# Attention's half of an up-projection in Strassen units, that half first in every pair but the first, and gate rows scaled in the input projection

## The chip, the cores and the metric

The kernel runs on one core of a Trainium2 chip. The core has five engines with a queue each, run in the order of the program: TensorE (PE, with its weight loads listed as PEld), VectorE (DVE), ScalarE (ACT), GpSimd (POOL) and SyncE (SP), which here issues most DMA transfers. The metric is the device time of one execution in microseconds, the median of several runs. Matmuls write to PSUM, eight banks of 128 partitions x 512 float32 values; everything else lies in SBUF or in DRAM.

## The reference: one decoder layer

Float32 throughout, 512 tokens, model width 2048. The part that matters:

```
proj = rmsnorm(x) @ w_in                 # u, v_sgu, q, k, v: 1024 wide each; g_a, g_b: 2048 wide
y_a  = chunked_spatial_gating(gelu(u), rmsnorm(gelu(v_sgu)))
y_b  = stick_breaking_attention(rmsnorm(q), rmsnorm(k), v)
merged = sigmoid(g_a) * (y_a @ w_up_a) + sigmoid(g_b) * (y_b @ w_up_b)
x = x + merged @ w_o
x = x + (silu(gate) * up) @ w_ffn_out    # gate, up = rmsnorm(x) @ w_ffn_in
x = x + sigmoid(rmsnorm(x) @ w_ple_gate) * (p @ w_ple)
```

The norm of x is a factor of each token; the kernel multiplies it to the columns of `proj` afterwards, as `row1`.

## The kernel before

**Operands and units.** TensorE multiplies numbers of fewer bits than float32 has, so each operand is split into a high and a low part (`hi`, `lo`), and each product is three matmuls, high by high, high by low, low by high (`mm3`, lines L296 to L298). Activations lie with the token as the free dimension. A *unit* is 256 rows by 256 columns of weights against 512 tokens. A plain unit ("P") is 4 weight blocks x 3 = 12 matmuls of 512 columns. A Strassen unit ("S") computes seven products of sums of quarters instead of eight, each on 256 tokens: 7 x 3 = 21 matmuls of 256 columns. Where all units of a pair are Strassen units, `doubled` merges two of the three matmuls into one of 512 columns (L692); the input projection does so for five of the seven products, w_o and the FFN for all.

**Pairs.** A *pair* is a column block of 256 outputs: units over all rows of the input, accumulated in PSUM. A plain pair leaves its two halves in two banks (`ends()`). A Strassen pair sums its products into an SBUF tile (`mix`, by ScalarE copies L748 and VectorE sums, or `mix_doubled`, L751 and others); a mixed pair, with both kinds, adds its plain units' banks to that (`rest`, L796).

**Weights.** They come unit by unit or as two units at once (a *double*), in four steps: the load by SP (a plain double 512 KB; of a Strassen one 256 and 384 KB, and another 256 KB that GpSimd's queue adds onto the first in SBUF, L363); the high part by ScalarE (`whi`, L359); two sums of 256 for each Strassen unit by VectorE (L375); the low part by VectorE (`wlo`, L356). Three slots hold split weights. `prepare_early` and `prepare_late` push the next doubles through these steps from places inside a unit.

**Operands' forms.** A *form* turns an activation block of 256 rows into what TensorE reads: its high part by ScalarE (L286), its low part by VectorE (L287), both writing `parts`. A plain form does this for 1024 values of each partition. A Strassen form (`late_form`) is made plain first (`plain_first`), used so in the first pairs, and loaded a second time for the sums of quarters (L527) that its Strassen products need; from the pair number in a list like `HALF` on, a unit is a Strassen unit. A form is built by `tick()`, a counter that goes on once or twice in a unit and lets work start that is due (`after(n, ...)`: in n ticks; WAIT = 2 ticks for a load).

**Stages.** Input projection until 815.28 us: 28 pairs over eight blocks of x, in four rounds of q, k, v and some gate pairs, then s and u (the gating part) among the last gates. Attention's steps and those of the gating run beside it, called by ticks: in attention, L1134 writes a low part that matmul L1141 (a product with a triangle of ones) reads. A gate pair's 256 columns are stored to DRAM (`gsp`) as they are. Up-projection, 815.28 to 1004.59 us: for each of eight j, first attention's half (`b`, y_b from DRAM by `w_up_b[j]`), then the gating's half (`a`, y_a in SBUF by `w_up_a[j]`), four plain units each; five pairs also compute the small embedding product (`w_ple`), a plain unit each. For each half, the gate comes back from DRAM, is scaled by `row1` (L1224) and goes through the sigmoid (L1357), and the two banks are multiplied to it (L1362). The sum of both goes to DRAM as `mix`. Then w_o (eight pairs over the eight `mix` blocks, the first plain, the second mixed), the FFN in and out, and the last gate.

The order of instructions on each engine comes from the order in which the program issues them, with weights' steps at a higher priority.

Of the kernel before, what the change touches and what calls it, by code (L numbers as in the profile page):

```python
# [29 lines left out]
EPS = 1e-6  # L30
MASKED = -1e4

PASSES = "SSSSSSSS", "SSSSSSSS", "SSSSPP"
HALF = 1, 1, 1, 1, 2, 2, 2, 2
PLAIN_UNTIL = HALF, HALF, (2, 2, 2, 2, 1, 1)
# [35 lines left out]
def hybrid_layer(  # L71
# [28 lines left out]
    def nm(s):  # L100
        return f"{s}_{next(names)}"
# [509 lines left out]
                    src, far)  # L611

    def plain_form(src, ready=always, gain=None, raw=1024, how="low", far=False):
        def steps(form):
            hi, lo = form.blocks = parts.take(1024, how), parts.take(1024, how)
            w = form.raw()
            if gain:
                gained(hi.own(), w.f(), *gain)
                gi, k = gain
                for i in range(2):  # L620
                    a, b = i * T, (i + 1) * T
                    nc.vector.scalar_tensor_tensor(
                        out=lo.own(a, b), in0=w.f(a, b),
                        scalar=gcol[:, gi + 2 * k + i : gi + 2 * k + i + 1], in1=hi.f(a, b),
                        op0=ALU.mult, op1=ALU.subtract)
            else:
                split_into(hi.own(), lo.own(), w.f())
            give(w)
            return tuple([x.own(0, T), x.own(T)] for x in form.blocks)
            yield  # L630

        return Form("P", steps, [(parts, 1024, how)] * 2 + [(wholes, raw, "low")] * bool(raw),
                    ready, src, far)

    class Pair:
# [555 lines left out]
    def sgu_v(rnd, o):  # L1191

        for h in range(2):
# [18 lines left out]
            for t in range(NT):  # L1212
# [5 lines left out]
                scalar=gcol[:, g_sgu + g : g_sgu + g + 1],  # L1218
                in1=bb.unsqueeze(1).to_broadcast([P, NT, P]),
                op0=ALU.mult, op1=ALU.add)  # L1220

    def scaled(o, row):
        b = o.rearrange("p (b t) -> p b t", t=T)
# [49 lines left out]

    def plan_rest():
        for j in range(KU):
            for b in "ba":
                plan((w_up_a if b == "a" else w_up_b)[j], "PPPP")
            if 0 < j < 6:
                planned.append((w_ple[j + 2].rearrange("p (b c) -> p b c", b=4), 1, "P"))
        for j in range(KU):  # L1280
# [9 lines left out]
            plan(w_gate[j], now(GATE, GATE_UNTIL, j))  # L1290

    def y_form(c, i):
        return plain_form((lambda: y_a[i]) if c == "a" else lambda: load(y_spill[i]),
                          lambda: len(y_done) == 8, raw=0 if c == "a" else 1024,
                          far=c == "b")

    ys = {(c, i): y_form(c, i) for c in "ba" for i in range(4)}
    build(ys.values())
    for n, ((w, i), pr) in enumerate(zip(order, made())):
        if n == 0:  # L1300
# [19 lines left out]
        elif w == "u":  # L1320
            scaled(o, row1)
            nc.scalar.activation(o, o, AF.Gelu_apprx_tanh)
            nc.vector.tensor_tensor(out=y_a[i].f(), in0=o, in1=y_a[i].f(), op=ALU.mult)
            y_done["a", i] = True
        else:
            d = tc.dram_tile([P, 1024], F32, name=nm("gsp"))
            nc.sync.dma_start(out=d, in_=o)
            gate_spill[w, i] = d
    finish_waiting()
    give(*att.values())  # L1330


    part = {}
# [14 lines left out]
    ms = [spilled_form("S", "mix", j) for j in range(KU)]  # L1348
    build(ms)
    for j in range(KU):  # L1350
        for b in "ba":
            s = load(gate_spill[b, j], 1024, "low")
            g = s.f()

            def gate(g=g):
                scaled(g, row1)
                nc.scalar.activation(g, g, AF.Sigmoid)  # L1357

            after(1, gate)
            pr = pair([ys[b, i] for i in range(4)], last=j == KU - 1)  # L1360
            for h, ps in zip((g[:, :T], g[:, T:]), pr.ends()):
                nc.vector.tensor_tensor(out=h, in0=h, in1=ps, op=ALU.mult)  # L1362
            if b == "b":
                part[j] = s
            else:
                nc.vector.tensor_tensor(out=g, in0=g, in1=part[j].f(), op=ALU.add)
# [4 lines left out]
        elif j < 6:  # L1371
            ple_pair(j + 2)
            if j == 5:
                ple_done()
    give(norm1.block)


    norm2 = Norm()
    fs = [spilled_form("S", "x1", j, (g_ffn, j)) for j in range(KU)]
# [194 lines left out]
```

## Time and profile before

| | |
|---|---|
| median of 3 runs | 2658.71 us (2658.05 to 2658.91) |
| the profiled execution | 2659.74 us |
| its span, first to last instruction | 2658.0 us |
| mean granted TensorE clock | 0.999 |
| input projection | 0 to 815.28 us |
| up-projection | 815.28 to 1004.59 us |
| DMA traffic | 559.77 MB, mean 211 GB/s |

In a row of the timeline stand the start and the duration in microseconds, engine and line, the operation with what it writes and reads, and in brackets the idle time of the engine ahead of it with the instruction that ended it. In a group of instructions the count is followed by the busy time in us, the mean duration in ns, and the idle time ahead of them. In the table by stretches each engine has its busy time and the number of instructions; then come the granted clock, the busy share of the DMA engines and the rate that they moved.

### The profile page before, as it was taken

The numbers are of one execution on the slowest core, as the hardware profiler recorded it, in microseconds if no ns is written. First come the engines' busy times: TensorE is split into PE (matmuls) and PEld (weight loads), VectorE is DVE, ScalarE is ACT, GpSimd is POOL, SyncE is SP. The second block draws the span as 40 slices with busy tenths as digits, with TensorE's granted clock in tenths as the row PEclk, the third lists the DMA queues.
The fourth block names the chain that finished last, engine by engine and source line by source line (L and its number), as shares of the span: only waits on it lengthen the run. The fifth ranks groups of instructions, "written<-read, shape, count | busy, mean of one in ns | idle before, by whom it ended". The sixth has DMA issues, their size and how long they took to land.

```text
span 2658.0 us, 42554 instructions
## 1 busy us (share of the span) xinstructions
PE 2638.2 (99%) x15336; PEld 2312.3 (87%) x15336; DVE 2234.6 (84%) x3821; ACT 1403.2 (53%) x2233; POOL 448.1 (17%) x556
## 2 busy tenths in 40 slices
PE   8999999999999999999999999999999999999999
PEld 7888888888998888888888888888888888889898
DVE  8687878787886558999888888888889989989876
ACT  7756565655554334566444444444445445455543
POOL 0122222232220001101111111111110211211110
PEclk9999999999999999999999999999999999999999
DMA  7677777777775668978888888788887989978884
GB/s 229 162 194 171 192 173 191 172 191 179 178 191 183 232 212 268 265 236 218 223 210 216 206 200 203 194 209 204 199 207 221 257 227 273 229 229 260 256 240 123
DMA packets 293459, 559.77 MB, mean 211 GB/s; under 512 B 26368, under 2 KB 140544, under 8 KB 293248
## 3 DMA queue, kind: packets, MB, share of 16 engines
q1 hardware_dynamic: 231136, 441.95, 50.7%
q0 software_dynamic: 62112, 115.11, 27.5%
q8 instruction: 120, 1.97, 0.3%
q14 instruction: 91, 0.75, 0.1%
HBM read 505.57 MB, written 51.38 MB: 210 GB/s over the span
## 4 chain that ended last, share of the span: by engine, by line
PE 90%; DVE 4%; DMA 3%; issue 1%; ACT 1%; SPq 0%; POOL 0%; ACTq 0%; POOLq 0%; DVEq 0%
PE ps L692 53%; PE ps L298 10%; PE ps L297 9%; PE ps L296 9%; PE small L692 6%; DVE wlo L356 1%; DVE wholes L527 1%; DMA wholes<-w_ffn_out 1%; PE small L1103 1%; PE small L1155 1%; DVE parts L287 1%; PE small L1029 1%; DMA x<-wholes 1%; ACT whi L359 0%; PE small L1214 0%
## 5 line engine op out<-in xcount | busy, mean ns | idle before, releaser
L692 PE MATMUL ps<-parts,whi 128*128 128x512 f32 x4200 | 1409.4, 398 | 1.6 <-DVE out L796 1.0
L359 ACT ACTIVATE whi<-wholes 128x512 fp32r<-128x512 f32 (+2 forms) x940 | 871.5, 941 | 745.8 <-DVE wholes L375 286.6
L356 DVE TENSOR_TENSOR wlo<-wholes,whi 128x512 fp32r<-128x512 f32 (+2 forms) x940 | 979.4, 1076 | 73.7 <-ACT whi L359 73.0
L692 PEld LDWEIGHTS ps<-parts,wlo 128*128 128x128 f32 x4200 | 790.2, 188 | 178.2 <-issue 1.9
L692 PE MATMUL ps<-parts,wlo 128*128 128x256 f32 x4200 | 831.3, 279 | 0.9 <-DVE wlo L356 0.9
L692 PEld LDWEIGHTS ps<-parts,whi 128*128 128x128 f32 x4200 | 677.1, 189 | 10.5 <-issue 3.6
L297 PE MATMUL ps<-parts,whi 128*128 128x256 f32 (+1 forms) x1832 | 605.0, 331 | 0.7 <-DVE parts L287 0.5
L298 PE MATMUL ps<-parts,wlo 128*128 128x256 f32 (+1 forms) x1832 | 604.9, 331 | 0.5 <-DVE wlo L356 0.5
L296 PE MATMUL ps<-parts,whi 128*128 128x256 f32 (+1 forms) x1816 | 597.3, 330 | 7.4 <-ACT parts L286 5.3
L297 PEld LDWEIGHTS ps<-parts,whi 128*128 128x128 f32 x1832 | 347.0, 189 | 39.0 <-DVE parts L287 2.7
L296 PEld LDWEIGHTS ps<-parts,whi 128*128 128x128 f32 x1816 | 343.6, 190 | 40.4 <-ACT parts L286 5.7
L298 PEld LDWEIGHTS ps<-parts,wlo 128*128 128x128 f32 x1832 | 347.3, 190 | 32.4 <-DVE wlo L356 1.6
L375 DVE TENSOR_TENSOR wholes<-wholes 128x256 f32<-128x256 f32 (+1 forms) x820 | 345.0, 421 | 17.9 <-DVE wlo L356 1.4
L751 DVE TENSOR_TENSOR out<-out,ps 128x256 f32<-128x256 f32 x490 | 202.3, 416 | 147.6 <-ACT out L748 147.4
L363 POOL DMA_DIRECT2D wholes<-w_ffn_in x169 | 147.1, 870 | 702.1 <-DVE wholes L375 251.7
L363 POOL DMA_DIRECT2D wholes<-w_in x132 | 116.6, 885 | 531.3 <-DVE wholes L375 132.8
L692 PE MATMUL small<-parts,whi 128*128 128x512 f32 x480 | 190.3, 397 | 0.0
L287 DVE TENSOR_TENSOR parts<-wholes,parts 128x1024 fp32r<-128x1024 f32 (+3 forms) x137 | 122.8, 907 | 18.5 <-ACT parts L286 18.5
L286 ACT ACTIVATE parts<-wholes 128x1024 fp32r<-128x1024 f32 (+3 forms) x137 | 106.5, 800 | 54.2 <-DVE wholes L527 35.7
L748 ACT ACTIVATE out<-ps 128x256 f32<-128x256 f32 x258 | 96.3, 383 | 50.7 <-PE ps L692 46.7
L363 POOL DMA_DIRECT2D wholes<-w_ffn_out x64 | 55.7, 871 | 360.6 <-DMA wholes<-w_ffn_out 89.2
L1402 ACT ACTIVATE out<-out 128x512 f32<-128x512 f32 x44 | 27.9, 633 | 155.6 <-DVE out L1401 155.6
(124 smaller groups left out, 1770.0 us busy)
## 6 DMA issues: line engine op xcount, KB each, us to landing
wholes<-w_ffn_in SPq DMA_DIRECT2D x169, 384.0 KB, 5.5
wholes<-w_in SPq DMA_DIRECT2D x132, 384.0 KB, 5.1
wholes<-w_ffn_in SPq DMA_DIRECT2D x169, 256.0 KB, 4.7
wholes<-w_ffn_in POOLq DMA_DIRECT2D x169, 256.0 KB, 5.3
wholes<-w_in SPq DMA_DIRECT2D x132, 256.0 KB, 4.3
wholes<-w_in POOLq DMA_DIRECT2D x132, 256.0 KB, 5.0
wholes<-w_ffn_out SPq DMA_DIRECT2D x64, 384.0 KB, 6.3
wholes<-x SPq DMA_DIRECT2D x45, 512.0 KB, 5.8
```

Source lines behind the costliest of these rows:

```text
L286: return (nc.scalar.activation(hi, src, AF.Copy), nc.vector.tensor_tensor(out=lo, in0=src, in1=hi.bitcast(F32), op=ALU.subtract))
L287: nc.vector.tensor_tensor(out=lo, in0=src, in1=hi.bitcast(F32), op=ALU.subtract))
L296: nc.tensor.matmul(ps, sh, mh, start=start, stop=False)
L297: nc.tensor.matmul(ps, sh, ml, start=False, stop=False)
L298: return nc.tensor.matmul(ps, sl, mh, start=False, stop=stop)
L356: in_turn(nc.vector.tensor_tensor(out=self.lo[:, blocks], in0=r, in1=h.bitcast(F32), op=ALU.subtract))
L359: in_turn(nc.scalar.activation(h, r, AF.Copy))
L363: nc.gpsimd.dma_start(out=raw[:, 3:5], in_=self.src[:, 1:3], accum_op=ALU.add)
L375: in_turn(nc.vector.tensor_tensor(out=o, in0=x, in1=y, op=ALU.add))
L692: m = nc.tensor.matmul(out, l, r, start=first and k == 0, stop=last and k == 1)
L748: in_turn(nc.scalar.activation(out, x, AF.Copy, scale=scale))
L751: in_turn(nc.vector.tensor_tensor(out=out, in0=x, in1=y, op=op))
```

## The change

- The four forms of y_b become Strassen forms, loaded a second time. `UP_UNTIL = 1, 1, 2, 2`: the first two units of attention's half are plain in pair j = 0 and Strassen units from j = 1 on, the other two from j = 2 on. So j = 0 is plain, j = 1 mixed, j = 2 to 7 all Strassen, not doubled.
- Pair j = 0 has the gating's half first, all others attention's half; weights are planned in the same order. y_a's forms are built first, the first of them with one block at the other end of the arena.
- A Strassen pair's sum lies in an SBUF tile, and the gate is multiplied with it in one instruction of 1024 values; before, two read the banks.
- A gate pair is scaled by `row1` before it is stored, two ticks after its sum is there; at its load only the sigmoid is left, two ticks later.
- The input projection no longer ends by running all waiting steps (`finish_waiting()`); attention's tiles are given back in the last round of `sgu_v`, and the norm's block three ticks later.

```diff
--- before.py
+++ after.py
@@ -30,6 +30,7 @@
 EPS = 1e-6
 MASKED = -1e4
 
+UP_UNTIL = 1, 1, 2, 2
 PASSES = "SSSSSSSS", "SSSSSSSS", "SSSSPP"
 HALF = 1, 1, 1, 1, 2, 2, 2, 2
 PLAIN_UNTIL = HALF, HALF, (2, 2, 2, 2, 1, 1)
@@ -611,8 +612,10 @@
                     src, far)
 
     def plain_form(src, ready=always, gain=None, raw=1024, how="low", far=False):
+        hows = [how] * 2 if isinstance(how, str) else how
+
         def steps(form):
-            hi, lo = form.blocks = parts.take(1024, how), parts.take(1024, how)
+            hi, lo = form.blocks = [parts.take(1024, h) for h in hows]
             w = form.raw()
             if gain:
                 gained(hi.own(), w.f(), *gain)
@@ -629,7 +632,7 @@
             return tuple([x.own(0, T), x.own(T)] for x in form.blocks)
             yield
 
-        return Form("P", steps, [(parts, 1024, how)] * 2 + [(wholes, raw, "low")] * bool(raw),
+        return Form("P", steps, [(parts, 1024, h) for h in hows] + [(wholes, raw, "low")] * bool(raw),
                     ready, src, far)
 
     class Pair:
@@ -1218,6 +1221,10 @@
                 scalar=gcol[:, g_sgu + g : g_sgu + g + 1],
                 in1=bb.unsqueeze(1).to_broadcast([P, NT, P]),
                 op0=ALU.mult, op1=ALU.add)
+        if rnd == 3:
+            assert ("b", 3) in y_done
+            give(*att.values())
+            att.clear()
 
     def scaled(o, row):
         b = o.rearrange("p (b t) -> p b t", t=T)
@@ -1273,8 +1280,9 @@
 
     def plan_rest():
         for j in range(KU):
-            for b in "ba":
-                plan((w_up_a if b == "a" else w_up_b)[j], "PPPP")
+            for b in "ba" if j else "ab":
+                plan((w_up_a if b == "a" else w_up_b)[j],
+                     "PPPP" if b == "a" else now("SSSS", UP_UNTIL, j))
             if 0 < j < 6:
                 planned.append((w_ple[j + 2].rearrange("p (b c) -> p b c", b=4), 1, "P"))
         for j in range(KU):
@@ -1290,11 +1298,14 @@
             plan(w_gate[j], now(GATE, GATE_UNTIL, j))
 
     def y_form(c, i):
-        return plain_form((lambda: y_a[i]) if c == "a" else lambda: load(y_spill[i]),
-                          lambda: len(y_done) == 8, raw=0 if c == "a" else 1024,
-                          far=c == "b")
-
-    ys = {(c, i): y_form(c, i) for c in "ba" for i in range(4)}
+        def ready():
+            return len(y_done) == 8
+
+        if c == "a":
+            return plain_form(lambda: y_a[i], ready, raw=0, how="low" if i else ("high", "low"))
+        return late_form(lambda size=1024: load(y_spill[i], size), ready, far=True)
+
+    ys = {(c, i): y_form(c, i) for c in "ab" for i in range(4)}
     build(ys.values())
     for n, ((w, i), pr) in enumerate(zip(order, made())):
         if n == 0:
@@ -1323,11 +1334,14 @@
             nc.vector.tensor_tensor(out=y_a[i].f(), in0=o, in1=y_a[i].f(), op=ALU.mult)
             y_done["a", i] = True
         else:
-            d = tc.dram_tile([P, 1024], F32, name=nm("gsp"))
-            nc.sync.dma_start(out=d, in_=o)
-            gate_spill[w, i] = d
-    finish_waiting()
-    give(*att.values())
+            d = gate_spill[w, i] = tc.dram_tile([P, 1024], F32, name=nm("gsp"))
+
+            def spill_gate(o=o, d=d):
+                scaled(o, row1)
+                nc.sync.dma_start(out=d, in_=o)
+
+            after(2, spill_gate)
+    after(3, lambda: give(norm1.block))
 
 
     part = {}
@@ -1348,19 +1362,18 @@
     ms = [spilled_form("S", "mix", j) for j in range(KU)]
     build(ms)
     for j in range(KU):
-        for b in "ba":
+        for b in "ba" if j else "ab":
             s = load(gate_spill[b, j], 1024, "low")
             g = s.f()
-
-            def gate(g=g):
-                scaled(g, row1)
-                nc.scalar.activation(g, g, AF.Sigmoid)
-
-            after(1, gate)
-            pr = pair([ys[b, i] for i in range(4)], last=j == KU - 1)
-            for h, ps in zip((g[:, :T], g[:, T:]), pr.ends()):
-                nc.vector.tensor_tensor(out=h, in0=h, in1=ps, op=ALU.mult)
-            if b == "b":
+            after(2, lambda g=g: nc.scalar.activation(g, g, AF.Sigmoid))
+            pr = pair([ys[b, i] for i in range(4)], last=j == KU - 1, j=j,
+                      until=UP_UNTIL if b == "b" else None)
+            if pr.n["S"]:
+                tt(g, g, pr.out(), ALU.mult)
+            else:
+                for h, ps in zip((g[:, :T], g[:, T:]), pr.ends()):
+                    tt(h, h, ps, ALU.mult)
+            if j not in part:
                 part[j] = s
             else:
                 nc.vector.tensor_tensor(out=g, in0=g, in1=part[j].f(), op=ALU.add)
@@ -1372,8 +1385,6 @@
             ple_pair(j + 2)
             if j == 5:
                 ple_done()
-    give(norm1.block)
-
 
     norm2 = Norm()
     fs = [spilled_form("S", "x1", j, (g_ffn, j)) for j in range(KU)]
```

Lines move by one to a few: L356 becomes L357, L692 L695, L748 L751, L796 L799, L1134 L1137, L1141 L1144, L1224 L1231, L1357 L1368. Three places of the instruction order follow, each before and after the change.

**Attention, first round.** VectorE ahead of the low part that L1141 reads (L1134, after the change L1137). `wlo` is the weights' low part, `out` the sum of a gate pair. Before:

```order
L1147 TENSOR_TENSOR wholes<-wholes,small_2722 128x384
L356 TENSOR_TENSOR wlo_79<-wholes,whi_78 128x1280
L356 TENSOR_TENSOR wlo_79<-wholes,whi_78 128x512
L1134 TENSOR_TENSOR parts<-wholes,parts 128x512
L1112 SCALAR_TENSOR_TENSOR wholes<-wholes 128x128
```

After:

```order
L1150 TENSOR_TENSOR wholes<-wholes,small_2725 128x384
L357 TENSOR_TENSOR wlo_79<-wholes,whi_78 128x1280
L357 TENSOR_TENSOR wlo_79<-wholes,whi_78 128x512
L1231 TENSOR_TENSOR out_2632<-out_2632,wholes 128x1024
L1137 TENSOR_TENSOR parts<-wholes,parts 128x512
L1115 SCALAR_TENSOR_TENSOR wholes<-wholes 128x128
```

The scaling of a gate now stands ahead of the low part. TensorE at the same place; `small` is the bank of the masked sums, `tri` the triangle, `ps` the input projection's banks. Before:

```order
L692 MATMUL ps_2706<-parts,whi_80 128x512
L692 MATMUL ps_2706<-parts,wlo_81 128x256 x2
L692 MATMUL ps_2706<-parts,whi_80 128x512
L692 MATMUL ps_2717<-parts,whi_80 128x512
L1141 MATMUL small_2802<-parts,tri_123 128x512
L692 MATMUL ps_2717<-parts,wlo_81 128x256 x2
L692 MATMUL ps_2717<-parts,whi_80 128x512
L692 MATMUL ps_2735<-parts,whi_80 128x512
L692 MATMUL ps_2735<-parts,wlo_81 128x256 x2
L692 MATMUL ps_2735<-parts,whi_80 128x512
```

After:

```order
L695 MATMUL ps_2709<-parts,whi_80 128x512
L695 MATMUL ps_2709<-parts,wlo_81 128x256 x2
L695 MATMUL ps_2709<-parts,whi_80 128x512
L695 MATMUL ps_2720<-parts,whi_80 128x512
L695 MATMUL ps_2720<-parts,wlo_81 128x256 x2
L695 MATMUL ps_2720<-parts,whi_80 128x512
L695 MATMUL ps_2738<-parts,whi_80 128x512
L695 MATMUL ps_2738<-parts,wlo_81 128x256 x2
L695 MATMUL ps_2738<-parts,whi_80 128x512
L1144 MATMUL small_2807<-parts,tri_123 128x512
```

The masked sum, L1141 and now L1144, has moved behind seven more matmuls.

**Start of the up-projection, ScalarE.** L286 (now L287) writes the high parts of operands, in the 1024 form those of plain forms; `whi` is the weights' high part. Before:

```order
L286 ACTIVATE parts_73<-wholes_74 128x1024
L359 ACTIVATE whi1_78<-wholes_74 128x1024
L286 ACTIVATE parts_73<-wholes_74 128x1024
L359 ACTIVATE whi0_76<-wholes_74 128x1024
L1357 ACT_TABLE_LOAD
L1357 ACTIVATE wholes_74<-wholes_74 128x1024
L286 ACTIVATE parts_73<-wholes_74 128x1024 x2
L359 ACTIVATE whi2_80<-wholes_74 128x1024
L286 ACTIVATE parts_73<-wholes_74 128x1024 x2
```

After:

```order
L287 ACTIVATE parts_73<-wholes_74 128x1024 x3
L360 ACTIVATE whi2_80<-wholes_74 128x1024
L751 ACTIVATE out_783_8229<-ps_777_8099 128x256
L751 ACTIVATE out_783_8229<-ps_778_8104 128x256
L751 ACTIVATE out_783_8229<-ps_779_8109 128x256
L751 ACTIVATE p5_784_8234<-ps_780_8118 128x256
L287 ACTIVATE parts_73<-wholes_74 128x4x256
L360 ACTIVATE whi1_78<-wholes_74 128x1024
L287 ACTIVATE parts_73<-wholes_74 128x4x256 x2
L360 ACTIVATE whi0_76<-wholes_74 128x1024
L287 ACTIVATE parts_73<-wholes_74 128x4x256
L1368 ACT_TABLE_LOAD
```

Before, the first four 1024-wide operands are attention's, with the load of the sigmoid's table (ACT_TABLE_LOAD) ahead of the last of the others. Now the gating's four (three of them shown) come first, before the input projection's last sums (L751), then attention's, written in the layout of Strassen forms (4x256), and the table behind them all.

**w_o, second to third pair.** VectorE; L796 (now L799) adds a mixed pair's banks to its sum. Before:

```order
L356 TENSOR_TENSOR wlo_81<-wholes,whi_80 128x1280
L356 TENSOR_TENSOR wlo_81<-wholes,whi_80 128x512
L287 TENSOR_TENSOR parts<-wholes,parts 128x3x256
L375 TENSOR_TENSOR wholes<-wholes 128x256
L287 TENSOR_TENSOR parts<-wholes,parts 128x256
L375 TENSOR_TENSOR wholes<-wholes 128x256
L287 TENSOR_TENSOR parts<-wholes,parts 128x256
L796 TENSOR_TENSOR out_9665<-ps_9648,out_9665 128x512
L356 TENSOR_TENSOR wlo_79<-wholes,whi_78 128x1280
L356 TENSOR_TENSOR wlo_79<-wholes,whi_78 128x512
L796 TENSOR_TENSOR out_9665<-ps_9641,out_9665 128x512
```

After:

```order
L357 TENSOR_TENSOR wlo_81<-wholes,whi_80 128x1280
L528 TENSOR_TENSOR wholes<-wholes 128x256
L357 TENSOR_TENSOR wlo_81<-wholes,whi_80 128x512
L288 TENSOR_TENSOR parts<-wholes,parts 128x3x256 x2
L376 TENSOR_TENSOR wholes<-wholes 128x256
L288 TENSOR_TENSOR parts<-wholes,parts 128x256
L376 TENSOR_TENSOR wholes<-wholes 128x256
L288 TENSOR_TENSOR parts<-wholes,parts 128x256
L357 TENSOR_TENSOR wlo_79<-wholes,whi_78 128x1280
L357 TENSOR_TENSOR wlo_79<-wholes,whi_78 128x512
L799 TENSOR_TENSOR out_10071<-ps_10054,out_10071 128x512
L799 TENSOR_TENSOR out_10071<-ps_10047,out_10071 128x512
```

Both sums now stand behind the low parts of `wlo_79`; before, one stood ahead of them. TensorE; `whi_76` and `whi_80` are the weights of the pair's first and second double, each group of three rows is one product. Before:

```order
L692 MATMUL ps_9835<-parts,whi_76 128x512
L692 MATMUL ps_9835<-parts,wlo_77 128x256 x2
L692 MATMUL ps_9835<-parts,whi_76 128x512
L692 MATMUL ps_9844<-parts,whi_76 128x512
L692 MATMUL ps_9844<-parts,wlo_77 128x256 x2
L692 MATMUL ps_9844<-parts,whi_76 128x512
L692 MATMUL small_9854<-parts,whi_76 128x512
L692 MATMUL small_9854<-parts,wlo_77 128x256 x2
L692 MATMUL small_9854<-parts,whi_76 128x512
L692 MATMUL ps_9814<-parts,whi_80 128x512
L692 MATMUL ps_9849<-parts,whi_76 128x512
```

After:

```order
L695 MATMUL ps_10232<-parts,whi_80 128x512
L695 MATMUL ps_10232<-parts,wlo_81 128x256 x2
L695 MATMUL ps_10232<-parts,whi_80 128x512
L695 MATMUL ps_10237<-parts,whi_80 128x512
L695 MATMUL ps_10237<-parts,wlo_81 128x256 x2
L695 MATMUL ps_10237<-parts,whi_80 128x512
L695 MATMUL ps_10248<-parts,whi_80 128x512
L695 MATMUL ps_10248<-parts,wlo_81 128x256 x2
L695 MATMUL ps_10248<-parts,whi_80 128x512
L695 MATMUL ps_10257<-parts,whi_76 128x512
L695 MATMUL ps_10257<-parts,wlo_77 128x256 x2
L695 MATMUL ps_10257<-parts,whi_76 128x512
```

Before, bank 9849 is used after five products of the first double; now the second double's products run on four banks ahead of 10257 and 10262.

## The prediction

> **What bounds the kernel now.** I read the page first: busy time, then the chain of work that ended last.
>
> ```profile
> span 2658.0 us, 42554 instructions
> PE 2638.2 (99%) x15336; PEld 2312.3 (87%) x15336; DVE 2234.6 (84%) x3821; ACT 1403.2 (53%) x2233; POOL 448.1 (17%) x556
> PE 90%; DVE 4%; DMA 3%; issue 1%; ACT 1%; SPq 0%; POOL 0%; ACTq 0%; POOLq 0%; DVEq 0%
> ```
>
> TensorE works 99% of the span and carries 90% of the chain. So the change is worth what it takes from TensorE, less the waits that it makes there. Next the busy time by stage: the up-projection (815.28 to 1004.60), its first microseconds, w_o behind it, and a stretch of the FFN.
>
> ```profile
> core 0: us, PE busy (x) PEld busy (x) DVE busy (x) ACT busy (x) POOL busy (x), PEclk, DMA share, GB/s
> 815.28:1004.60 189.32, 188.57 (x831) 155.27 (x830) 110.00 (x120) 72.40 (x79) 0.88 (x1) 1.00 0.62 210
> 820.00:830.00 10.00, 9.25 (x39) 6.73 (x38) 8.22 (x8) 8.51 (x9) 0.00 (x0) 1.00 0.82 263
> 1004.60:1060.00 55.40, 54.43 (x295) 46.84 (x293) 50.30 (x85) 29.80 (x38) 7.04 (x8) 1.00 0.92 279
> 1100.00:1200.00 100.00, 100.00 (x558) 86.78 (x557) 93.31 (x162) 60.64 (x87) 12.62 (x14) 1.00 0.86 250
> ```
>
> In the up-projection VectorE is busy 58% and DMA moves 210 GB/s; in the FFN TensorE has no gap at all with VectorE at 93% and DMA at 250 GB/s. These two are the covers I measure the added work against.
>
> **The change, part by part.**
>
> *TensorE.* A plain unit is 12 matmuls of 512 columns, a Strassen unit 21 of 256. Durations of single matmuls overlap, so I take the pitch, start to start, from the timeline:
>
> ```profile
> 815.28 0.40 PE L296 MATMUL ps<-parts,whi 128*128 128x512 f32 x1
> 1004.59 0.39 PE L296 MATMUL ps<-parts,whi 128*128 128x512 f32 x1
> 1010.25 0.39 PE L297 MATMUL ps<-parts,whi 128*128 128x512 f32 x1
> 1025.89 0.39 PE L297 MATMUL ps<-parts,whi 128*128 128x512 f32 x1
> 1026.46 0.28 PE L297 MATMUL ps<-parts,whi 128*128 128x256 f32 x1
> 1031.50 0.28 PE L297 MATMUL ps<-parts,whi 128*128 128x256 f32 x1
> ```
>
> The third and fourth rows lie 69 matmuls apart: 15.64/69 = .2267 us for 512 columns. The last two lie 42 apart: 5.04/42 = .1200 us for 256, each with a weight load of its own. A plain unit costs 2.720 us, a Strassen unit 2.520. Units of attention's half that change: the first two of each pair from pair 1 on (7 + 7), the others from pair 2 on (6 + 6), 26 in all. One more 512-column matmul of the mixed pair is halved into two. So 313 × .2267 leave and 548 × .1200 come: 70.95 − 65.76 = **−5.2 us**.
>
> [...]
>
> *The hole at the start.* The stage holds 64 plain units and 5 of the small embedding product, 69 × 12 = 828 matmuls, 187.7 us by the pitch; it takes 1004.59 − 815.28 = 189.3. So 1.6 us of holes, nearly all here:
>
> ```profile
> 826.23 0.39 PE L298 MATMUL ps<-parts,wlo 128*128 128x512 f32 x1
> 826.85 0.73 PE L296 MATMUL ps<-parts,whi 128*128 128x512 f32 x2 [0.22 <-ACT parts L286]
> 828.11 0.50 PE L297 MATMUL ps<-parts,whi 128*128 128x512 f32 x1 [0.53 <-DVE parts L287]
> 828.44 0.39 PE L298 MATMUL ps<-parts,wlo 128*128 128x512 f32 x1
> ```
> ```profile
> 810.14 1.06 ACT L286 ACTIVATE parts<-wholes 128x1024 fp32r<-128x1024 f32 x1 [4.29 <-DMA wholes<-y]
> 821.46 1.06 ACT L286 ACTIVATE parts<-wholes 128x1024 fp32r<-128x1024 f32 x1 [3.58 <-DMA wholes<-y]
> 823.49 1.28 ACT L1357 ACT_TABLE_LOAD   x1
> 825.75 1.99 ACT L286 ACTIVATE parts<-wholes 128x1024 fp32r<-128x1024 f32 x2
> ```
>
> Four steps took 2.21 us instead of .91. ScalarE builds attention's operands first, waits for y loads between them (4.29 and 3.58 us), loads the sigmoid table, and reaches the other half's operands, which need no load, when TensorE is already there. The change starts with that half and builds its operands in the last pair of the input projection; attention's loads then have the first pair's 4 × 2.72 = 10.9 us as added cover. I take the whole hole, **−1.6** (bounds −1.6 and 0).
>
> *Loads at the start.* Against that, attention's operands are now loaded twice (plain first, then for the Strassen sums): 4 more loads of 512 KB. Two of them, with their sums, must be there at pair 1's attention half, 2 × 10.9 = 21.8 us into the stage. DMA already moves 263 GB/s at 820 to 830, and the most of any row is 279. A load waited for costs ScalarE at most 4.29 us above. Walking through the stage with 5 to 6 us for a load and VectorE's sums in line, I find about 2 us of slack, too thin to be sure of: **+0.5** (bounds 0 and +4.3).
>
> Over the whole stage each of the 13 Strassen doubles brings 384 + 256 + 256 KB where a plain one brings 512: +384 KB × 13 = 5.0 MB, with the reloads 7.1 MB on 189.3 us × 210 GB/s = 39.8 MB. That is 257 GB/s over some 182.5 us, just above the 250 at which 1100 to 1200 has no gap: 0, but without reserve.
>
> *VectorE in the up-projection.*
>
> ```profile
> L356 DVE TENSOR_TENSOR wlo<-wholes,whi 128x1280 fp32r<-128x1280 f32 x404 | 600.7, 1487 | 22.6 <-ACT whi L359 22.2
> L356 DVE TENSOR_TENSOR wlo<-wholes,whi 128x512 fp32r<-128x512 f32 x442 | 303.3, 686 | 15.7 <-ACT whi L359 15.7
> L356 DVE TENSOR_TENSOR wlo<-wholes,whi 128x1024 fp32r<-128x1024 f32 x82 | 100.1, 1221 | 35.3 <-ACT whi L359 35.1
> L375 DVE TENSOR_TENSOR wholes<-wholes 128x256 f32<-128x256 f32 x808 | 341.6, 423 | 17.7 <-DVE wlo L356 1.4 <-issue 1.1
> L287 DVE TENSOR_TENSOR parts<-wholes,parts 128x768 fp32r<-128x768 f32 x38 | 36.2, 951 | 3.4 <-ACT parts L286 3.4
> L1224 DVE TENSOR_TENSOR wholes<-wholes 128x1024 f32<-128x1024 f32 x20 | 24.4, 1222 | 20.5 <-DMA wholes<-gsp 20.5
> L1362 DVE TENSOR_TENSOR wholes<-wholes,ps 128x512 f32<-128x512 f32 x32 | 21.4, 685 | 19.9 <-PE ps L298 13.3 <-ACT wholes L1357 6.6
> ```
>
> Weights' low parts: 13 × (1.487 + .686 − 1.221) = +12.4. Their sums: 26 × .423 = +11.0. Mixing the products of 7 pairs: 5 sums of 256 and one of 512 from PSUM, then one product of 1024 in SBUF where two from PSUM stood: 5 × .423 + .685 + 1.222 − 2 × .685 = 2.65 each, +18.5. Second parts of four operands, four sums, a 768 and a 256 each: 4 × (4 × .423 + .951 + .423) = +12. Gate scaling gone: 16 × 1.222 = −19.6. Together 110 + 34 = 144 of 182.5 us, 79%, under the 93% above: **0**. ScalarE and GpSimd stay lower still.
>
> *Gate scaling in the input projection.* The 16 scalings of 1.22 us now stand among attention's steps, and in each of the four rounds one stands directly ahead of the low part (L1134) that a masked sum of TensorE (L1141) waits for:
>
> ```profile
> 279.06 0.67 DVE L1134 TENSOR_TENSOR parts<-wholes,parts 128x512 fp32r<-128x512 f32 x1
> 280.23 0.39 PE L1141 MATMUL small<-parts,tri 128*128 128x512 f32 x1
> ```
>
> The low part ends at 279.73, .50 ahead of its use. Late by 1.22 it would hold TensorE .72, in four rounds 2.9 us. But the order of the changed program puts that matmul seven places later: three of 512 and four of 256, 3 × .2267 + 4 × .1200 = 1.16. Since 1.22 − .50 − 1.16 is below 0: **0** (bounds 0 and +2.9).
>
> *w_o, second to third pair.* TensorE waits here for the last sums (L796) of a pair, which free its banks:
>
> ```profile
> 1049.74 0.68 DVE L796 TENSOR_TENSOR out<-ps,out 128x512 f32<-128x512 f32 x1
> 1050.34 2.08 DVE L356 TENSOR_TENSOR wlo<-wholes,whi 128x1280 fp32r<-128x1280 f32 x2
> 1050.48 0.50 PE L692 MATMUL ps<-parts,whi 128*128 128x512 f32 x1 [0.17 <-DVE out L796]
> 1053.17 0.47 PE L692 MATMUL ps<-parts,whi 128*128 128x512 f32 x1 [0.80 <-DVE out L796]
> ```
>
> .17 + .80 = 1.0 us. In the changed order both sums stand behind the 2.08 us of low parts, and one more operand's second part falls in this pair: later by 2 to 4 us. TensorE in turn runs eight products of the next double (8 × (.2267 + .1200) = 2.8 us) before it needs these banks. The two cancel within a microsecond: **0** (bounds −1.0 and +1.5).
>
> *The sum.* −5.2 − 1.6 + 0.5 = −6.3 us. The profiled execution took 2659.74 (the span and 1.7 outside it), 1.0 above the median of the runs; it would come to 2653.4, and the median to 2658.7 − 6.3 = 2652.4. I say **2652.5**. Its own range, from the bounds that leave the mechanism whole: 2650.9 (−5.2 − 1.6 − 1.0) to 2655.5 (−5.2, the hole filled by 0.5 of 1.6, +1.5 in w_o).
>
> **Rivals.**
>
> *A. Gate scaling holds TensorE in attention.* For it: only .50 us of slack, and VectorE's queue is in program order. Against it: the later place of the matmul. 2652.4 + 2.9 = 2655.3.
>
> *B. The start becomes bound by loads (slower).* Until pair 1's attention half, 21.8 us in, SP issues up to 2.1 MB of reloads and .4 MB more weights, in one queue with the weights of the next pairs. At 279 GB/s that is 9.0 us of transfer; the room above 263 is 16 GB/s × 21.8 us = .35 MB, 1.3 us. TensorE would wait 7.7 us. A wait also costs clock:
>
> ```profile
> 630.00:640.00 10.00, 8.08 (x56) 7.28 (x54) 6.37 (x10) 3.89 (x12) 2.81 (x3) 1.00 0.91 237
> 640.00:650.00 10.00, 9.69 (x54) 8.87 (x55) 6.17 (x12) 6.84 (x19) 1.21 (x2) 0.83 0.50 97
> PE small L1214 <- ACT wholes L1052: 2.2, 1, 2.2
> ```
>
> After a wait of 2.2 us the granted clock is .83 over the next 10 us: .17 × 10 = 1.7 us lost. So 2651.9 (the sum without its +0.5) + 7.7 + 1.7 = 2661.3. It turns slower than before from 5.1 us of waiting on. For it: 263 GB/s, and ScalarE's y waits. Against it: the stage's mean of 210 GB/s, so that reloads for pair 2 can come later.
>
> [...]
>
> [...]
>
> *D. Weight loads bound the Strassen units:* loading takes longer than the pitch of 256.
>
> ```profile
> L298 PEld LDWEIGHTS ps<-parts,wlo 128*128 128x128 f32 x1832 | 347.3, 190 | 32.4 <-DVE wlo L356 1.6
> ```
>
> If loads did not overlap, 546 × (.190 − .120) = +38 us: 2690. Against it: the even .120 includes them.
>
> *E. Waits elsewhere shift away:* the stall before 640 us (2.2 + 1.7 = 3.9) goes, as all orders around it move a little: 2648.5. Against it: the instructions there keep their order.
>
> **How the numbers follow.** Forecast .62, A .14, B .11, C .03, D .02, E .08. A measurement of this kernel can tell about 0.2%, 5.3 us, so "faster" ends at 2653.4. The forecast lies just beyond it: of its .62, .48 falls faster and .14 same. B as priced is 0.1% slower, which is same (.05); in the other .06 its waits come again in pair 2, whose reloads stand in the same queue, and pass 2664.0. Faster: .48 + .03 (C) + .08 (E) = .59. Same: .14 + .14 (A) + .05 = .33. Slower: .06 + .02 (D) = .08. The range reaches down to C and up beyond A, and leaves out most of E below and B and D above, some .19: 2649.5 to 2657.5.
>
> **What would show it.** Right: the up-projection takes about 182.5 us from its first to w_o's first matmul; a Strassen unit 2.52; no wait at the start of the second pair; VectorE near 79% and DMA near 257 GB/s there; L1141's matmuls without a wait on VectorE; w_o's waits about 1 us. Wrong: a wait on operands or on y loads at 837 us (B), waits of about .7 us in each attention round (A), a pitch other than .120 (C, D). A saving much above 7.8 us would mean that a wait left some stage that I have taken as unchanged.

## The result and the profile after

The changed kernel takes 2664.01 us (median of 22 runs, 2658.81 to 2671.57), the kernel before 2659.02 (22 runs, 2657.06 to 2665.12): a ratio of 1.0019, 95% interval 1.0013 to 1.0025. It is slower by 5.0 us where 6.3 us of gain were forecast, and lies outside the predicted range. Its runs also spread wider.

The profiled execution happens to be the fastest of the 22, 2658.81 us, so it shows less than the median's loss. Its page, first lines and chain:

```profile
span 2656.9 us, 43242 instructions
PE 2633.3 (99%) x15571; PEld 2316.4 (87%) x15571; DVE 2278.1 (86%) x3915; ACT 1423.7 (54%) x2266; POOL 452.0 (17%) x569
PE 88%; DVE 4%; DMA 4%; ACT 2%; issue 1%; POOL 0%; SPq 0%; POOLq 0%; ACTq 0%; DVEq 0%
```

TensorE works 4.9 us less (2638.2 before), nearly the 5.2 forecast, but the span is only 1.1 us shorter, and in the chain DMA and ScalarE have each gained 1%. The stages, by the table of stretches (up-projection; w_o up to its 351st matmul; two places of waits):

```profile
core 0: us, PE busy (x) PEld busy (x) DVE busy (x) ACT busy (x) POOL busy (x), PEclk, DMA share, GB/s
811.92:1002.49 190.57, 185.02 (x1065) 162.63 (x1064) 132.30 (x194) 88.62 (x110) 10.80 (x13) 1.00 0.73 235
1002.49:1071.35 68.86, 64.86 (x351) 55.64 (x350) 60.79 (x100) 35.19 (x44) 8.60 (x10) 1.00 0.93 284
882.00:892.00 10.00, 7.64 (x59) 7.24 (x60) 8.50 (x10) 6.84 (x10) 0.00 (x0) 1.00 0.28 92
1020.00:1040.00 20.00, 16.56 (x112) 14.89 (x111) 19.64 (x33) 10.92 (x12) 2.63 (x3) 1.00 0.85 253
```

The up-projection takes 190.57 us where 182.5 were forecast, although VectorE is busy only 132 us of it and DMA moves 235 GB/s, both below the covers of the prediction. Two waits of each kind, from TensorE's timeline:

```profile
883.26 0.38 PE L297 MATMUL ps<-parts,whi 128*128 128x256 f32 x1 [1.56 <-ACT whi L360]
884.78 0.39 PE L299 MATMUL ps<-parts,wlo 128*128 128x256 f32 x1 [1.02 <-DVE wlo L357]
1023.60 0.50 PE L298 MATMUL ps<-parts,whi 128*128 128x512 f32 x1 [1.68 <-DVE parts L288]
1034.89 0.38 PE L298 MATMUL ps<-parts,whi 128*128 128x256 f32 x1 [1.76 <-DVE parts L288]
```

In the up-projection TensorE waits for weights' high parts (L360), then for the low parts behind them (L357): 5.3 us in six places between 883 and 982. With the pitch disturbed around them the stage lies 8.1 us over the pure pitches (515 × .2267 + 548 × .1200 = 182.5). In w_o it waits for the low parts of operands (L288), at the first pair's last operand and in the second pair. The hole at the second pair, near 826 before, has no row any more. What ScalarE did ahead of 883:

```profile
872.33 0.61 ACT L360 ACTIVATE whi<-wholes 128x512 fp32r<-128x512 f32 x1
880.99 1.06 ACT L1368 ACTIVATE wholes<-wholes 128x1024 f32<-128x1024 f32 x1 [8.04 <-DMA wholes<-gsp]
881.95 2.94 ACT L360 ACTIVATE whi<-wholes 128x1280 fp32r<-128x1280 f32 x3
```

ScalarE stood 8 us at the sigmoid (L1368) of a gate whose load had not landed, with the weights' high parts behind it in its queue. That is the first theory, G: the gate's load holds ScalarE. SyncE's queue, and behind it two rows of the table by stretches, show why the load was late:

```profile
862.15 0.38 SPq L342 DMA_DIRECT2D wholes<-w_up_b  x1
862.58 0.49 SPq L344 DMA_DIRECT2D wholes<-w_up_b  x1
863.16 0.38 SPq L887 DMA_DIRECT2D ple<-out  x1
863.60 0.75 SPq L519 DMA_DIRECT2D wholes<-gsp  x1
864.44 0.81 SPq L342 DMA_DIRECT2D wholes<-w_up_b  x1
865.29 1.30 SPq L344 DMA_DIRECT2D wholes<-w_up_b  x1
866.68 0.45 SPq L519 DMA_DIRECT2D wholes<-mix  x1
867.23 0.44 SPq L340 DMA_DIRECT2D wholes<-w_up_a  x1
867.93 0.33 SPq L519 DMA_DIRECT2D wholes<-gsp  x1
```
```profile
870.00:875.00 5.00, 5.00 (x24) 4.14 (x23) 0.69 (x1) 1.58 (x2) 0.42 (x1) 1.00 1.00 323
875.00:880.00 5.00, 5.00 (x24) 4.14 (x23) 1.58 (x3) 0.00 (x0) 0.47 (x1) 1.00 0.97 302
```

The gate's load is the last of nine transfers issued in 6 us, and the sigmoid starts on its data 13 us later (880.99 − 867.93). From 870 to 880 us the DMA engines are 97 to 100% busy and move 302 to 323 GB/s. So the burst fills them, although the stage's mean of 235 GB/s lies below the prediction's cover of 250.

### The profile page after: what moved, and what is told of

It is laid out like the page before. It is cut to its first block, busy times and chain, and to the rows that moved or that the text cites. A ratio compares the mean times of both kernels' runs of the same rounds, so it can differ in the third digit from the quotient of the medians.

```text
span 2656.9 us, 43242 instructions
## 1 busy us (share of the span) xinstructions
PE 2633.3 (99%) x15571; PEld 2316.4 (87%) x15571; DVE 2278.1 (86%) x3915; ACT 1423.7 (54%) x2266; POOL 452.0 (17%) x569
## 4 chain that ended last, share of the span: by engine, by line
PE 88%; DVE 4%; DMA 4%; ACT 2%; issue 1%; POOL 0%; SPq 0%; POOLq 0%; ACTq 0%; DVEq 0%
PE ps L695 53%; PE ps L299 9%; PE ps L298 9%; PE ps L297 9%; PE small L695 6%; DVE wlo L357 2%; DMA wholes<-w_up_b 1%; DVE wholes L528 1%; PE small L1158 1%; ACT whi L360 1%; DMA wholes<-gsp 1%; PE small L1106 1%; PE small L1032 1%; DMA wholes<-mix 1%; DVE parts L288 0%
## 5 line engine op out<-in xcount | busy, mean ns | idle before, releaser
L695 PE MATMUL ps<-parts,whi 128*128 128x512 f32 x4200 | 1404.0, 397 | 0.7 <-DVE out L799 0.6
L360 ACT ACTIVATE whi<-wholes 128x512 fp32r<-128x512 f32 (+2 forms) x953 | 881.8, 939 | 701.6 <-DVE wholes L376 309.9
L357 DVE TENSOR_TENSOR wlo<-wholes,whi 128x512 fp32r<-128x512 f32 (+2 forms) x953 | 989.7, 1074 | 43.5 <-ACT whi L360 42.7
L695 PEld LDWEIGHTS ps<-parts,wlo 128*128 128x128 f32 x4200 | 788.6, 188 | 178.9 <-issue 1.9
L695 PE MATMUL ps<-parts,wlo 128*128 128x256 f32 x4200 | 830.8, 279 | 0.1
L695 PEld LDWEIGHTS ps<-parts,whi 128*128 128x128 f32 x4200 | 676.1, 189 | 7.4 <-issue 1.8
L298 PE MATMUL ps<-parts,whi 128*128 128x256 f32 (+1 forms) x1910 | 615.7, 323 | 3.6 <-DVE parts L288 3.6
L299 PE MATMUL ps<-parts,wlo 128*128 128x256 f32 (+1 forms) x1910 | 616.1, 323 | 3.0 <-DVE wlo L357 2.8
L297 PE MATMUL ps<-parts,whi 128*128 128x256 f32 (+1 forms) x1893 | 608.2, 322 | 9.4 <-ACT parts L287 5.2
L298 PEld LDWEIGHTS ps<-parts,whi 128*128 128x128 f32 x1910 | 362.2, 190 | 37.8 <-DVE parts L288 5.2
L297 PEld LDWEIGHTS ps<-parts,whi 128*128 128x128 f32 x1893 | 358.6, 190 | 39.2 <-ACT whi L360 6.2
L299 PEld LDWEIGHTS ps<-parts,wlo 128*128 128x128 f32 x1910 | 362.4, 190 | 32.2 <-DVE wlo L357 5.3
L376 DVE TENSOR_TENSOR wholes<-wholes 128x256 f32<-128x256 f32 (+1 forms) x846 | 355.4, 420 | 25.7 <-DMA wholes<-w_up_b 8.3
L695 PE MATMUL small<-parts,whi 128*128 128x512 f32 x480 | 190.3, 397 | 0.0
L287 ACT ACTIVATE parts<-wholes 128x1024 fp32r<-128x1024 f32 (+3 forms) x143 | 110.9, 798 | 44.3 <-DVE wholes L528 37.2
L288 DVE TENSOR_TENSOR parts<-wholes,parts 128x1024 fp32r<-128x1024 f32 (+3 forms) x143 | 127.7, 904 | 6.8 <-ACT parts L287 6.7
L751 ACT ACTIVATE out<-ps 128x256 f32<-128x256 f32 x258 | 96.9, 386 | 52.5 <-PE ps L695 48.9
```

Of the source, the lines that this page charges most:

```text
L287: return (nc.scalar.activation(hi, src, AF.Copy), nc.vector.tensor_tensor(out=lo, in0=src, in1=hi.bitcast(F32), op=ALU.subtract))
L288: nc.vector.tensor_tensor(out=lo, in0=src, in1=hi.bitcast(F32), op=ALU.subtract))
L297: nc.tensor.matmul(ps, sh, mh, start=start, stop=False)
L298: nc.tensor.matmul(ps, sh, ml, start=False, stop=False)
L299: return nc.tensor.matmul(ps, sl, mh, start=False, stop=stop)
L357: in_turn(nc.vector.tensor_tensor(out=self.lo[:, blocks], in0=r, in1=h.bitcast(F32), op=ALU.subtract))
```

## The experiments

The rival theory, here called D (it is not the prediction's rival D), was that Strassen weights, with three transfers and two sums to wait for, land too late whatever stands in ScalarE's queue. Medians below are of 6 to 12 runs, ratios against the kernel before on the same chip; the runs were made on three chips. "Stage" is the up-projection from its first matmul to w_o's first, in one profiled execution of each kernel, of "before" and of the change in two. The last column is for the 16 sigmoids of this stage.

| kernel | median, us | ratio (95%) | stage, us | ScalarE idle ahead of the sigmoid, us |
|---|---|---|---|---|
| before, twice | 2659.5 (second) | 1.0002 (.9993 to 1.0010) | 189.31, 188.73 | 44.8 (first) |
| the change, again | 2666.32 | 1.0027 (1.0017 to 1.0038) | 190.57 (first), 191.68 | 65.4 (first) |
| plain | 2658.13 | .9998 (.9990 to 1.0007) | 187.71 | 22.7 |
| strassen | 2667.84 | 1.0040 (1.0027 to 1.0054) | 188.11 | 44.9 |
| early | 2654.86 | .9988 (.9980 to .9997) | 183.04 | 23.9 |
| sig4 | 2654.21 | .9985 (.9976 to .9993) | 182.66 | 28.7 |
| mixlate | 2661.06 | 1.0005 (.9996 to 1.0014) | 182.68 | 50.3 |
| early_half | 2654.55 | .9984 (.9975 to .9993) | 182.70 | |
| sig4_half | 2655.54 | .9990 (.9981 to .9999) | 184.31 | |

**The change once more.** 

> The changed kernel once more, for another execution's trace. Theory G (a gate's load holds ScalarE: the sigmoid stands ahead of the weights' high parts in its queue and waits for the load) and theory D (Strassen weights land too late, whatever stands in ScalarE's queue) both expect waits for weights of 4 to 9 us in the up-projection and a median near 2664. If the 5 us by which the median lies above the first profiled execution are clock, a granted clock under 1.00 shows in the 10 us after such waits, 1.7 us for each; if they are waits alone, the clock stays at 1.00 and the waits are longer.

Its profiled execution took 2666.16 us, nearer to the median. Waits for weights: 5.0 us, near 888 and 916. And the clock fell, by the table of stretches of that execution:

```profile
910.00:920.00 10.00, 7.23 (x31) 5.89 (x31) 5.77 (x9) 4.80 (x6) 0.00 (x0) 0.81 0.39 115
920.00:930.00 10.00, 10.00 (x74) 10.00 (x74) 6.18 (x7) 3.31 (x5) 0.89 (x1) 0.85 0.68 204
1030.00:1040.00 10.00, 9.22 (x54) 8.42 (x55) 10.00 (x15) 5.69 (x7) 0.89 (x1) 0.83 0.76 231
```

.19, .15 and .17 of 10 us: 5.1 us of clock withheld behind the waits, none in the first execution, where the waits were as long in sum. From 918.20 to 922.89 matmuls of 256 columns start .213 us apart instead of .120. Of the 3.4 us in the up-projection a part fell into the waits themselves and cost no time: the stage is only 1.1 us longer than in the first execution. Another 3.4 us were withheld near 20 and 640 us, places of waits that the kernel before has too. So clock can be a part of the wider spread; how large a part, two executions do not show.

**Without Strassen units.** 

> The change without Strassen units: attention's half in plain units, but the new order of the halves, the gate scaling in the input projection and all else kept. G and D: no late weights, the hole at the second pair gone, so 1.6 us below before, about 2657.4, with waits under 1 us in the up-projection. Rival A (the gate scaling holds TensorE in attention): 2659 or more, with waits of about .7 us at each of the four rounds.

```diff
-                     "PPPP" if b == "a" else now("SSSS", UP_UNTIL, j))
+                     "PPPP")
-        return late_form(lambda size=1024: load(y_spill[i], size), ready, far=True)
+        return plain_form(lambda: load(y_spill[i]), ready, far=True)
...
-            pr = pair([ys[b, i] for i in range(4)], last=j == KU - 1, j=j,
-                      until=UP_UNTIL if b == "b" else None)
+            pr = pair([ys[b, i] for i in range(4)], last=j == KU - 1)
```

The stage takes 187.71 us, to .03 the 828 matmuls at their pitch: the hole is gone, no weights are late, and no row shows the masked sums (L1144) waiting. So order and gate scaling cost TensorE nothing in these places, and gain 1.0 to 1.6 us in the stage. The median shows no gain that its interval would resolve.

**Gates loaded one half ahead.** 

> The change with each half's gate loaded one half ahead (5 to 10 us earlier), nothing else changed. G: ScalarE no longer waits for gates, the waits for weights in the up-projection fall from 5.3 us to under 1.5, and the median comes down by 5 to 8 us, to 2656 to 2659. D: the same waits of 4 to 9 us, median 2662 to 2666.

```diff
+    halves = deque((b, j) for j in range(KU) for b in ("ba" if j else "ab"))
+    coming = deque([load(gate_spill[halves.popleft()], 1024, "low")])
     for j in range(KU):
         for b in "ba" if j else "ab":
-            s = load(gate_spill[b, j], 1024, "low")
+            s = coming.popleft()
+            if halves:
+                coming.append(load(gate_spill[halves.popleft()], 1024, "low"))
```

No wait of TensorE is left in the stage: 183.04 us. The median falls by 11.5 us against the change on the same chip, to .9988, below the 2656 to 2659 that G gave. D expected 2662 to 2666 and falls. But G's first sign came only in part. ScalarE's idle time ahead of the sigmoids falls from 65.4 to 23.9 us, and in it stands one hold longer than the change's 8.04 us:

```profile
879.47 1.06 ACT L1372 ACTIVATE wholes<-wholes 128x1024 f32<-128x1024 f32 x1 [10.68 <-DMA wholes<-gsp]
880.43 2.94 ACT L360 ACTIVATE whi<-wholes 128x1280 fp32r<-128x1280 f32 x3
```

It cost TensorE nothing, because it ended in time: the high part behind it starts 66.9 us into the stage (880.43 − 813.48), in the change 70.0 us (881.95 − 811.92). So what counted here was when a hold ended, and not how long it was.

**Strassen units alone.** 

> The kernel before with Strassen units in attention's half alone: old order of the halves, gates scaled by VectorE after their load. G: VectorE now waits for the gate and ScalarE's sigmoid for VectorE, weights are late as well, and the hole at the second pair stays: 2662 to 2668. If it was the moved scaling that made the weights late, the saving of 5.2 us shows: about 2654.

The edit is, on the kernel before, the change's own lines on `UP_UNTIL`, `late_form`, the weights' plan, the pair and its sum. The median meets G's number, but not by G's road: waits for weights are only 1.4 us, the hole is there (1.3 us of waits), 1.7 + .5 us of waits near 606 are new, and w_o takes 70.4 us to its 351st matmul (65.6 before). With the scaling at the load, ScalarE's idle time ahead of the sigmoids is 44.9 us, as before the change (44.8) and a third less than 65.4. So the longer hold came with the rest of the change. The other expectation, that the saving shows as 2654, falls as well. Where the whole 9.2 us by which this median lies above the kernel before come from, the one profiled execution does not show.

**The sigmoid two ticks later.** 

> The change with the sigmoid asked for two ticks later. The loads, GpSimd's and VectorE's instructions keep their order; on ScalarE the sigmoid of attention's gate in the pairs from j = 2 on now stands behind the high parts of one more double instead of ahead of them. G (ScalarE held by the gate's load): the waits for whi at about 883 and 910 us and the waits for wlo right behind them go, 4.6 us with 1 to 2 us for starting again, and the clock lost behind them: median 2657 to 2660. D (Strassen weights late by themselves): waits stay at 4 us or more, median 2662 to 2666.

```diff
-            after(2, lambda g=g: nc.scalar.activation(g, g, AF.Sigmoid))
+            after(4, lambda g=g: nc.scalar.activation(g, g, AF.Sigmoid))
```

The narrowest test, since no load moves: through this stage the traces of the change and of this kernel have the instructions of SyncE, VectorE and GpSimd in the same order, and only ScalarE's order differs. The same place of ScalarE's timeline:

```profile
873.10 0.61 ACT L360 ACTIVATE whi<-wholes 128x512 fp32r<-128x512 f32 x1
878.93 1.28 ACT L360 ACTIVATE whi<-wholes 128x1280 fp32r<-128x1280 f32 x1 [5.22 <-DMA wholes<-w_up_b]
880.72 0.63 ACT L360 ACTIVATE whi<-wholes 128x512 fp32r<-128x512 f32 x1 [0.52 <-DVE wholes L376]
881.26 1.04 ACT L1368 ACTIVATE wholes<-wholes 128x1024 f32<-128x1024 f32 x1
```

The high part goes at 878.93, as soon as its weights are there, 3.0 us ahead of 881.95 in the change, though this stage began .9 us later; the sigmoid behind it no longer waits. In the same table as above, of this kernel, the stage has no gap:

```profile
812.85:995.51 182.66, 182.66 (x1065) 162.42 (x1064) 133.83 (x195) 89.31 (x110) 11.43 (x13) 1.00 0.77 248
```

TensorE is busy all of the 182.66 us. The median is 5.0 us below before, 2654.21, more than G expected. D, which expected 4 us or more of waits, does not hold: the same weights, loaded in the same order, are in time.

**Operands of w_o fetched later.** 

> The change with the operands of w_o fetched only from the fifth pair of the up-projection on; so up to four loads of 512 KB fewer stand in SP's queue ahead of gates in pairs 1 to 4. If these loads make the gates late: ScalarE's waits for gates before 930 us halve (from 5 to 8 us each) and the waits for whi there fall under 1 us; w_o's wait for its operands grows to 4 us or more. If the gates are late by the weights' bytes: no change before 930 us.

```diff
+    there, open_now = set(), [False]
...
-            lambda size=1024: load(spill[n, j], size), lambda: (n, j) in there, gain, far=True,
+            lambda size=1024: load(spill[n, j], size), lambda: (n, j) in there and open_now[0], gain, far=True,
...
+        open_now[0] = open_now[0] or j >= 4
```

The second sigmoid of a pair, which waited 8.04 and 6.70 us in the change's pairs 2 and 3, waits 3.21 and 2.81; the first still waits 5 to 6. No weights are late, stage 182.68, though ScalarE is still held 50.3 us in all: without the `mix` load just ahead of it in SyncE's queue the gate lands early enough. The other half of the expectation fails: w_o takes 65.5 us to its 351st matmul and waits .3 for an operand. The median is no better than before. In this execution waits of 1.4 us at 2097 and 1.2 at 2501 stand that the sig4 version doesn't have, and the input projection ends late (815.63); why the FFN has them was not tried.

**Fewer Strassen operands in w_o's second pair.** 

> The version with gates loaded one half ahead, and in w_o two more units plain in the second pair (HALF = 1, 1, 2, 2, 2, 2, 2, 2), so that two fewer operands need their Strassen sums there. If w_o's wait of 2.1 us at 1026 us is the late sums of mix operands: it goes, .4 us come by the two plain units, so 1 to 2 us below the early version, 2653 to 2654. If the wait is VectorE's queue as such: it moves into the third pair and the median stays at 2655 or above.

> The version with the sigmoid two ticks later and w_o's second pair with two more plain units (HALF = 1, 1, 2, 2, 2, 2, 2, 2). If the late sums of mix operands make w_o's wait of 1.8 us at 1026 us and the clock lost behind it: it goes, a wait of about 1 us for the last sums (L799) comes near 1047 us instead, the two plain units cost .4 us; 0 to 2 us below the sigmoid version, 2652.5 to 2654.5. The up-projection stays at 182.7 us. If that wait is covered elsewhere anyway: the same median, 2654 or above.

```diff
-HALF = 1, 1, 1, 1, 2, 2, 2, 2
+HALF = 1, 1, 2, 2, 2, 2, 2, 2
```

In both, the wait for L288 at the second pair goes, and a wait for L799 comes at the third: 1.08 us in the one execution, 2.19 with a granted clock of .83 behind it in the other. The medians lie .3 us below and 1.3 above those without the edit, which were taken on other chips; the ratios differ by less than their intervals: no gain is shown. The expected place was right, the gain not. In sig4_half the up-projection takes 184.31 us where 182.7 were expected, with .47 us of waiting for a low part at 916; the profiled execution was the slowest of the twelve, 2664.59 us.

**The kernel before, once more.** 

> The kernel before as a second look at its own trace: the up-projection at 189.3 us within .3, its hole of about 1.3 us at the second pair again, and in the input projection a stage end that moves by 1 to 3 us with the stall at 640 us, so that single looks at that stage tell nothing of less than 3 us. Against the kernel before: ratio 1.000 within .0008.

Ratio 1.0002. Its stage is 188.73, beyond the .3 allowed: the four steps of the hole took 1.89 us instead of 2.21, so it was 1.0 us and not 1.3. The stall at 640 was .5 us (2.2 before), and the stage began at 812.91 (815.28 before): single executions differ by 2.4 us in the input projection.

## Why the prediction was wrong

**Where the 5.0 us are.** Over two executions each, the stage takes 191.1 us (190.57, 191.68) against 189.0 (189.31, 188.73), and w_o from its first matmul to the start of the 351st on record 68.7 in both against 65.6 (65.2, 65.9): 2.1 + 3.1 = 5.2 us, near the 5.0 of the medians. But the four executions as a whole differ by only 2.3 us (2662.5 against 2660.1 on average), since behind these pairs the kernel before waited 1.9 and 5.4 us in its two and the change .4 and .9. What the other stages add to the medians, two executions each do not tell.

- **TensorE's saving, −5.2: right.** From plain to sig4 the stage falls by 187.71 − 182.66 = 5.05 us, and there TensorE is busy throughout. No run shows matmuls of 256 columns faster than the pitch of .1200, which the prediction's .03 for C and the lower end of its range count on: sig4's 182.66 us are the 182.5 of the two pitches within .2. So the prediction's C and D are out.
- **The hole, −1.6: right in the stage**, 1.0 to 1.6 by the two executions of before.
- **Loads at the start, +0.5:** no matmul between the stage's start and 860 us waits in the change. 0.
- **"257 GB/s over some 182.5 us, just above the 250 at which 1100 to 1200 has no gap: 0, but without reserve", and for VectorE and ScalarE "79%, under the 93% above: 0": the step that failed.** Instead of 0 it cost 8 us in the stage (190.57 − 182.66 = 7.9). The means were near enough (248 GB/s, and 134 us of VectorE where 144 were forecast, in sig4, which has no gap), but means do not price a queue. Taking the 16 scalings off VectorE was booked as −19.6 us of its time; it was not asked what then stands first at the gate's load. It is the sigmoid, with the next weights behind it. Two groups of ScalarE in this stage, before and after:

```profile
L359 ACT ACTIVATE whi<-wholes 128x1024 fp32r<-128x1024 f32 (+1 forms) x37 | 36.8, 998 | 51.7 <-PE ps L297 38.7 <-issue 12.1 <-DMA wholes<-w_o 0.9
L1357 ACT ACTIVATE wholes<-wholes 128x1024 f32<-128x1024 f32 x16 | 16.9, 1059 | 44.8 <-DVE wholes L1224 44.8
```
```profile
L360 ACT ACTIVATE whi<-wholes 128x1024 fp32r<-128x1024 f32 (+2 forms) x50 | 46.9, 953 | 20.1 <-DMA wholes<-w_up_b 7.1 <-DVE wholes L376 6.9 <-PE ps L298 3.1
L1368 ACT ACTIVATE wholes<-wholes 128x1024 f32<-128x1024 f32 x16 | 16.9, 1059 | 65.4 <-DMA wholes<-gsp 65.4
```

Before, ScalarE also lost 44.8 us to gates, harmlessly: its high parts mostly waited for TensorE to free a slot (38.7 us), so weights ran ahead. After, that reserve is 3.1 us; the high parts wait for loads and sums, and a hold of ScalarE that ends late reaches TensorE. A small reserve alone did no harm: in sig4 the same wait for TensorE is 6.1 us, with 17.1 us for loads, and the stage has no gap. The prediction could have read both rows of before. ScalarE did not take up the weights behind the sigmoid during its 8.04 us at 880.99: VectorE summed that double at 878.42 (L376), its high part began at 881.95; in sig4, ahead of the sigmoid, at 878.93.
- **Gate scaling in attention, 0: right**; A is out.
- **w_o, 0 (−1.0 to +1.5): wrong in place and size, +3.1.** The late work was seen ("one more operand's second part falls in this pair"), but priced only where it delays L796. The new waits are earlier, for low parts of operands (L288): 1.68 and 2.19 us at the last operand of the first pair, 1.76 and .35 at an operand of the second. The first all but goes with the sigmoid two ticks later (.20), the second stays (1.76) and goes with two more plain units in that pair. Without Strassen units in the up-projection (plain) both are absent. Which work ahead of them makes the second one late was not isolated.
- **B had the mechanism, loads that come late and cost wait and clock, at the wrong place:** not attention's operands at 837 us but gates from 870 on, 5 us of waits and none to at most 5.1 of clock instead of 7.7 and 1.7.
- **E:** the stall before 640 us was 2.2 and .5 us in two executions before, none and 1.7 in two after: not the change's.
- **A slip in the sum:** the upper end of the prediction's own range, 2655.5, does not follow from the terms named for it, which give 2658.7 − 5.2 − 0.5 + 1.5 = 2654.5. The stated range does not hang on it.

## What to carry to other kernels

Before adding loads or weights' work to a stage, look at what the splitting engine waits for. Before the change that was mostly TensorE (38.7 us): weights ran ahead, and 44.8 us of holds made no weights late. After it, with 3.1 us for TensorE and 7.1 and 6.9 us for loads and sums, a sigmoid that waited 8.04 us for its transfer delayed the weights behind it, and TensorE stopped for 1.56 and 1.02 us. Compare the time at which the hold ends with the time at which the weights behind it are used. Where an edit takes an instruction off the front of a load, ask which instruction stands there now, and what is queued behind it. Loading gates one half ahead (.9988), or the sigmoid two ticks later (.9985), beats both kernels, by .12 and .15% against the kernel before, with the intervals above.

## What the runs showed of the hardware

Waits of about the same length at the same place are followed by a lower granted clock in some executions and not in others. At w_o's second pair, the wait and the stretch around it in early, then in sig4:

```profile
1026.38 0.39 PE L298 MATMUL ps<-parts,whi 128*128 128x256 f32 x1 [2.06 <-DVE parts L288]
1020.00:1030.00 10.00, 7.94 (x64) 7.56 (x64) 7.83 (x14) 4.46 (x5) 1.74 (x2) 1.00 1.05 351
```
```profile
1026.43 0.39 PE L298 MATMUL ps<-parts,whi 128*128 128x256 f32 x1 [1.76 <-DVE parts L288]
1020.00:1030.00 10.00, 8.24 (x57) 7.93 (x56) 9.71 (x17) 5.94 (x7) 1.74 (x2) 0.86 0.96 294
```

The longer wait left the clock at 1.00, the shorter one at .86. Likewise at the last operand of w_o's first pair: in the change's first execution 1.68 us there left it at 1.00, in the other 2.19 us were followed by .83. Each loss near .83 is 1.7 us (.17 × 10 us). What decides between the two, these runs do not show.
